# Moving eight gate columns of a decoder layer from the opening projection to the value projection of the forgetting heads

## The chip, the core and the metric

The kernel runs on one core of a Trainium2 chip. The metric is the device time of one execution in microseconds (us). A core has a matrix unit (TensorE, PE in the profile, with its weight loads as PEld), three engines for everything elementwise (VectorE or DVE, ScalarE or ACT, GpSimd or POOL) and SyncE (SP), which here issues the loads of weights and inputs. Matmul results land in PSUM, in banks of 2 KB per partition; there are eight of them. Everything else lies in SBUF, 128 partitions wide. Each engine works off its own instructions in order and waits on semaphores for the others.

## The reference

One decoder layer for 512 tokens, model width 1024: two attention branches on the same modulated input, a gated merge, an output projection, and a gated MLP with a depthwise convolution. The part that matters here:

```python
mod = c @ w_ada + b_ada                       # six vectors of 1024: shifts, scales, gates
u = x * (1.0 + sc1) + sh1
proj = u @ w_in
q_a, k_a, v_a, f_a, q_b, k_b, v_b, g_a, g_b = jnp.split(proj, ...)   # a: forgetting, b: stick-breaking

log_f = jax.nn.log_sigmoid(f_a + b_forget)    # 8 columns of proj, one for each forgetting head
cum = jnp.cumsum(log_f, axis=-1)              # along the tokens
logits = q_a k_a^T / 8 + cum[q] - cum[k]      # causal, then softmax and times v_a: forgetting attention
...                                           # b: stick-breaking attention, strictly causal
merged = sigmoid(g_a) * (y_fox @ w_fox_proj) + sigmoid(g_b) * (y_sb @ w_sb_proj)
x = layer_norm(ALPHA * x + (1.0 + gt1) * (merged @ w_o), ln1_g, ln1_b)
...                                           # gated MLP on x * (1 + sc2) + sh2, second layer norm
```

`f_a` is 8 columns wide. These are the "gate columns" below: the logits of the forget gate. The heads are 64 wide, eight of each kind.

## The kernel before

**Products.** All matrix products are float32 in accuracy: each operand is split into a high part (a rounded copy, on ScalarE: `hi_of`, L100) and a low part (the difference, on VectorE: `lo_of`, L103), and each product is three matmuls, high by high, high by low, low by high. Names end in h and l accordingly: `uh`/`ul` (the modulated input u, transposed, 8 tiles of 128 model rows by 512 tokens), `wh`/`wl` (weights). `mm3` (L140) issues the three.

**The opening.** Eight steps j, one for each 128 rows of the model width. SP loads for each step two tiles `wa` (128x1024 columns of w_ada), one `w1` tile `raw` (six bias columns, then 904 weight columns: q, k and q of the first stick-breaking heads, 3 x 128, the 512 value columns of the stick-breaking heads, 8 gate columns) and `xt` (128x512 of x). VectorE makes two sums over `wa` times c (`mod_col`, L216, with an addition of a bias column each, L211 and L212; POOL copies the bias columns to `bcols`, L285), ScalarE makes `uh` from `xt` (L302), and x itself turns into u in place (L304); VectorE subtracts for `wl` and `ul`. TensorE adds each step into eight groups `grp[0..7]`, one for each of the eight PSUM banks, which stay open over all eight steps: groups 0 to 2 are q, k, q (three matmuls each, weights standing still, 512 tokens moving), groups 3 to 6 the four token blocks by 512 value columns (three each), and group 7 the gate logits, two matmuls each: there the standing operand is `fpad[:, j, :]`, 128 columns, with the high parts of the gate columns in columns 0 to 7, the low parts in 64 to 71 and zeros elsewhere. So a step has 23 matmuls of 512 columns (L330). In the last step the groups that are wanted first are finished first, and groups 2 and 7 come between the first scores.

**Behind the opening.** Attention heads come in the order of `PAIRS`: four pairs of stick-breaking heads, then four of forgetting heads. TensorE's work between a head's steps is taken from one long list, `stream`: projections of q and k of later pairs (`proj`), the value projection of the forgetting heads (`vproj`, four token blocks of 24 matmuls of 512 columns, just ahead of pair 4, the first forgetting pair), the branch gates, the branch projections. `fill(n)` takes n matmuls or so from it, `fill_to(mark)` all up to a mark. The weights of these come as `items` of 128x1024 in four `raw` buffers, and are split to high and low when their turn nears; the value weights are four such items (`v_proc`), each of two 512-column tiles. A pool `z` of 60 buffers of 2 KB per partition serves most tiles.

**The gate.** `forget_evac`, right behind the opening, copies group 7 out of PSUM: rows 64 to 71 and rows 0 to 7 (with b_forget added) to two tiles `fq` of 8 rows by 512 tokens. While the seventh head runs (n == 6), `forget` adds the two, forms log sigmoid as min(x, 0) plus Ln(Sigmoid(Abs(x))) and the running sum with a scan, and splits it into the tile `chi`. From there POOL issues the transfers of `decay_rows`: for each forgetting head, its two rows of `chi` to rows 66 and 67 of `s2t[n]` and to rows 64 and 65 of `m2t[n]`. These two tiles are operands of the head's second score products: `scores` (L522 and L523) takes for each group of query blocks a first product of `s1` and `m1` (128 rows: high q twice against high and low k) and a second of `s2` and `m2` (64 rows and the four extra ones, whose products add cum[q] - cum[k] to the logits). The rows 0 to 63 of `s2t` come from `s1` by a transfer that POOL issues too.

**What sets the order.** SP's loads stand in the order written. For the other engines the order comes from the list scheduler, from estimated times; where `chain` is on (in the opening and up to the second head's scores), the instructions of an engine stay in the order of the program, through the wrapper `Pinned`, whose calls carry line L70. `tc.issue_after` puts an instruction behind another one.

## Time and profile before

| | |
|---|---|
| median of 3 runs | 754.06 us (753.83 to 754.61) |
| profiled execution, its own time | 753.64 us |
| its span in the trace | 751.5 us |
| mean granted TensorE clock | 0.997 |
| busy: PE, DVE, ACT, POOL | 99%, 73%, 47%, 17% of the span |
| moved by DMA | 100.46 MB, 134 GB/s on average |
| opening's matmuls | 179 at L330 and 5 at L70, of 3502 |

The span runs from the first to the last instruction that the profiler recorded; the execution's own time is 2.1 us more. Rows of a timeline give the start in the span, the length, the engine, the line, the operation, its result and operands (result<-operands), the tile of weights (partitions x columns) where there is one, shapes and the count; in square brackets stands the idle time ahead of the row and what ended it. Rows of groups give the line, engine, operation, tiles, count, the shortest, mean and longest in ns and the time of the first and last. L103 or L140 are lines of helpers, so that such rows are told apart by their tiles. A window's row gives for TensorE, its weight loads, VectorE, ScalarE, POOL and SP the busy time and the count, then TensorE's clock, the share of the DMA engines that was busy and GB/s.

### The profile page before, as it was taken

To read this page: it belongs to the slowest core of one execution; us is meant where nothing else is said; L and a number is where in the kernel's file an instruction comes from. 1 tells how busy PE (TensorE), PEld (TensorE's weight loads), DVE (VectorE), ACT (ScalarE), POOL (GpSimd) and SP (SyncE) were. 2 spreads that over 40 slices of the span, in tenths; PEclk is the share of its full clock that TensorE was granted. 3 is DMA by queue.
4 is the path that set the end of the run, shared out by engine and by line. 5 is a ranking of instruction groups with operands and counts; after the bars stand their busy time and mean duration, and the time that the engine had idled before them with its cause. 6 is when DMAs were issued, how large, how long until landed. Compare 5 with 4: busy or idle time off the path is not lost.

```text
span 751.5 us, 9515 instructions
## 1 busy us (share of the span) xinstructions
PE 741.8 (99%) x3502; PEld 621.0 (83%) x3502; DVE 545.4 (73%) x896; ACT 351.9 (47%) x587; POOL 126.6 (17%) x153
## 2 busy tenths in 40 slices
PE   9999999999999999999999999999999999999995
PEld 7888888888888888888898888888888888888885
DVE  7888989867688875596987787666755686334666
ACT  5578767468655754343246344444444442212300
POOL 2103000030110000000000690000000137454400
PEclk9999999999999999999999999999999999999998
DMA  9941332424333434565234524333333234224102
GB/s 352 405 142 70 99 139 87 157 84 168 106 114 120 154 113 168 169 232 165 86 113 140 168 94 131 139 114 133 120 117 107 85 110 149 104 86 140 56 33 79
DMA packets 31088, 100.46 MB, mean 134 GB/s; under 512 B 4113, under 2 KB 4641, under 8 KB 31042
## 3 DMA queue, kind: packets, MB, share of 16 engines
q1 hardware_dynamic: 29536, 97.69, 37.3%
q0 software_dynamic: 1504, 2.17, 1.2%
q8 instruction: 27, 0.44, 0.2%
q14 instruction: 19, 0.16, 0.1%
q10 hardware_dynamic: 2, 0.00, 0.0%
HBM read 96.63 MB, written 2.11 MB: 131 GB/s over the span
## 4 chain that ended last, share of the span: by engine, by line
PE 97%; DVE 2%; DMA 0%; ACT 0%; issue 0%; DVEq 0%
PE ps L140 56%; PE ps L330 5%; PE ps L1086 5%; PE ps L1084 5%; PE ps L1085 5%; PE ps L613 3%; PE ps L70 2%; PE ps L585 2%; PE ps L795 2%; PE ps L796 2%; PE ps L794 2%; PE ps L523 1%; PE ps L522 1%; PE ps L496 1%; PE ps L497 1%; PE ps L498 1%
## 5 line engine op out<-in xcount | busy, mean ns | idle before, releaser
L103 DVE TENSOR_TENSOR wl<-raw,wh 128x1024 fp32r<-128x1024 f32 (+1 forms) x99 | 133.2, 1346 | 55.4 <-ACT wh L100 55.2
L140 PE MATMUL ps<-u2h,wh 128*128 128x512 f32 (+1 forms) x376 | 141.2, 376 | 0.0
L140 PE MATMUL ps<-u2l,wh 128*128 128x512 f32 (+1 forms) x376 | 141.0, 376 | 0.0
L140 PE MATMUL ps<-u2h,wl 128*128 128x512 f32 (+1 forms) x376 | 133.6, 376 | 0.0
L100 ACT ACTIVATE wh<-raw 128x1024 fp32r<-128x1024 f32 (+1 forms) x99 | 103.5, 1048 | 62.7 <-PE ps L1086 46.1
L140 PE MATMUL ps<-uh,wh 128*128 128x512 f32 x213 | 84.1, 395 | 0.0
L140 PE MATMUL ps<-ul,wh 128*128 128x512 f32 x213 | 83.3, 391 | 0.0
L140 PEld LDWEIGHTS ps<-u2h,wh 128*128 128x128 f32 x376 | 70.8, 188 | 12.9
L140 PEld LDWEIGHTS ps<-u2l,wh 128*128 128x128 f32 x376 | 70.8, 188 | 12.6
L140 PEld LDWEIGHTS ps<-u2h,wl 128*128 128x128 f32 x376 | 70.4, 188 | 12.9
L140 PE MATMUL ps<-uh,wl 128*128 128x512 f32 x213 | 78.9, 390 | 0.0
L683 POOL TENSOR_TENSOR raw<-raw,gt 128x1024 f32<-128x1024 f32 x22 | 56.4, 2571 | 92.6 <-DMA raw<-in_wdn 85.0
L1057 DVE SCALAR_TENSOR_TENSOR cv<-ps,cw,cv 128x511 f32<-128x511 f32 x44 | 32.9, 748 | 53.4 <-ACT cv L1056 53.4
L1056 ACT ACTIVATE cv<-ps,cw 128x512 f32<-128x512 f32 x44 | 34.1, 776 | 45.7 <-PE ps L140 45.7
L1084 PE MATMUL ps<-wh,hh 128*128 128x512 f32 x128 | 49.8, 389 | 0.0
L1085 PE MATMUL ps<-wl,hh 128*128 128x512 f32 x128 | 49.8, 389 | 0.0
L1086 PE MATMUL ps<-wh,hl 128*128 128x512 f32 x128 | 49.8, 389 | 0.0
L140 PEld LDWEIGHTS ps<-uh,wl 128*128 128x128 f32 x213 | 40.0, 188 | 8.7
L140 PEld LDWEIGHTS ps<-uh,wh 128*128 128x128 f32 x213 | 40.0, 188 | 8.0
L140 PEld LDWEIGHTS ps<-ul,wh 128*128 128x128 f32 x213 | 40.1, 188 | 7.9
L100 ACT ACTIVATE hh<-cv 128x512 fp32r<-128x512 f32 x22 | 13.9, 633 | 57.5 <-DVE cv L1064 57.5
L216 DVE SCALAR_TENSOR_TENSOR ada<-ada,cbc 128x1024 f32<-128x1024 f32 x24 | 29.3, 1219 | 9.1 <-DMA ada<-in_wa 8.7
(245 smaller groups left out, 1428.7 us busy)
## 6 DMA issues: line engine op xcount, KB each, us to landing
raw<-in_wup SPq DMA_DIRECT2D x44, 512.0 KB, 3.4
raw<-in_wct SPq DMA_DIRECT2D x29, 512.0 KB, 3.8
ada<-in_wa SPq DMA_DIRECT2D x24, 512.0 KB, 4.3
raw<-in_wdn SPq DMA_DIRECT2D x22, 512.0 KB, 3.3
wa<-in_wa SPq DMA_DIRECT2D x16, 512.0 KB, 7.4
raw<-in_wp SPq DMA_DIRECT2D x8, 512.0 KB, 3.3
raw<-in_wo SPq DMA_DIRECT2D x8, 512.0 KB, 4.0
raw<-in_wa SPq DMA_DIRECT2D x8, 512.0 KB, 3.3
```

What stands on the lines that cost most here:

```text
L100: S.activation(o, i, AF.Copy, scale=scale)
L103: return V.tensor_tensor(o, i, fl(hi), ALU.subtract)
L140: PE.matmul(ps, w, u, start=first and n == 0, stop=last and n == 2)
L216: V.scalar_tensor_tensor(wt, wt, 1.0, cbc, ALU.mult, ALU.mult, accum_out=raw)
L330: PE.matmul(grp[g], w, u, start=j == 0 and n == 0, stop=j == KT - 1 and n == (1 if g == 7 else 2))
L613: PE.matmul(ps[:, to : to + w], v_part(br, h, j), src[e][:, so : so + w], start=a == 0 and j == 0, stop=a == 1 and j == 3)
L683: G.tensor_tensor(r, r, gt[1], ALU.mult)
L1056: S.activation(t, ps, AF.Identity, bias=cw[:, n, 3:4], scale=cw[:, n, 2:3])
L1057: V.scalar_tensor_tensor(t[:, 1:], ps[:, 0:511], cw[:, n, 1:2], t[:, 1:], ALU.mult, ALU.add)
L1084: PE.matmul(ps, hh[j][:, tb], w[0], start=first, stop=False)
L1085: PE.matmul(ps, hh[j][:, tb], w[1], start=False, stop=False)
L1086: PE.matmul(ps, hl[j][:, tb], w[0], start=False, stop=last)
```

## The change

The eight gate columns leave `w1` (`W1C` 904 to 896). They go into the value weights of the forgetting heads: each row of `wv` is now 256 value columns, 8 gate columns, 256 value columns (`VW` = 520), and the loads, the four `raw` buffers and the split tiles widen accordingly. Group 7 and `fpad` are gone, and with them the two gate matmuls of each step, the small copy on ScalarE and the small subtraction on VectorE; a tile of zeros `zpad` takes the place of `fpad` in the first two matmuls of the program. Of the two sums over `wa` for step j + 1, sum 0 moves ahead of `ul` of step j (`mod_sum` and `mod_add` are now apart). Among the scores of the first head stands group 6 instead of group 7.

`vproj` now takes each token block in two halves, of 264 and of 256 columns, each with 24 matmuls and a PSUM bank of its own; ScalarE copies the last 8 columns of the first half (tokens by heads, 128x8) to a tile `fgt`. `forget_evac` becomes an item of the stream, behind q of pair 4: four TensorE transposes turn `fgt` into heads by tokens in one PSUM bank, and ScalarE copies 8 rows of it with the bias to rows 96 to 103 of `chi`, which is now 104 rows by 512; the two `fq` are rows 64 and 96 of it, the high rows 0 to 7 and the low rows 32 to 39. The addition of the two parts is gone; the rest of `forget` is as it was. The memsets of the two `m2z` tiles are written ahead of the opening.

```diff
-W1C = 904
+W1C = 896
+VW = 512 + 8
-NZ = 60
+NZ = 59
-    fpad = early.tile([P, KT, P], F32R, name="fpad", tag="fpad")
+    zpad = early.tile([P, 512], F32R, name="zpad", tag="zpad")
...
-            it[3] = stg.tile([P, 1024], F32, name=nm("raw"), tag="raw", bufs=LOADS)
+            it[3] = stg.tile([P, 2 * VW], F32, name=nm("raw"), tag="raw", bufs=LOADS)
...
     def first_acc(j):
         wa = pend[j][0]
         G.tensor_copy(bcols[:, :, j], pend[j][2][:, 0:6])
-        mod_col(0, j, wa[0])
-        return mod_col(2, j, wa[1])
+        if j == 1:
+            mod_sum(0, j, wa[0])
+        mod_sum(2, j, wa[1])
+        mod_add(0, j)
+        return mod_add(2, j)
...
     def first_mod(j):
-        state["after"] = lo_of(b, xt, a)
-        with tc.issue_after(state["after"].ins):
-            hi_of(fpad[:, j, 0:NH], r[:, f])
-            state["pad"] = lo_of(fpad[:, j, 64 : 64 + NH], r[:, f], h[:, f])
+        if j + 1 < KT:
+            with tc.issue_after(state["split"].ins):
+                early_sum = mod_sum(0, j + 1, pend[j + 1][0][0])
+            with tc.issue_after(early_sum.ins):
+                state["after"] = lo_of(b, xt, a)
+        else:
+            state["after"] = lo_of(b, xt, a)
...
     def first_ops(j, g):
-        if g == 7:
-            return [(fpad[:, j, :], a), (fpad[:, j, :], b)]
...
+    m2z = [z(F32R, "m2z", (68, 512)) for _ in range(2)]
+    for t in m2z:
+        G.memset(fl(t[64:68, :]), 0.0)
+
     for j in range(2):
         first_load(j)
...
-            first_mm(j, range(5, 8))
+            first_mm(j, range(5, 7))
         else:
-            first_mm(j, (0, 1, 3, 4, 5, 6))
+            first_mm(j, (0, 1, 3, 4, 5))
...
-        chi.append(att.tile([NH, 2, 512], F32R, name="chi", tag="chi"))
+        chi.append(att.tile([96 + NH, 512], F32R, name="chi", tag="chi"))
...
+    def forget_open():
+        fgt.append(atp[0].tile([P, NB * NH + P], F32, name="fgt", tag="fgt"))
+        G.memset(fgt[0][:, NB * NH :], 0.0)

     def forget_evac():
-        S.activation(fq[0], grp[7][64 : 64 + NH, :], AF.Copy)
-        S.activation(fq[1], grp[7][0:NH, :], AF.Identity, bias=bfs)
+        fq.extend(fl(chi[0][r : r + NH, :]) for r in (64, 96))
+        ps = bank()
+        for j in range(NB):
+            PE.transpose(ps[:, j * P : (j + 1) * P], fgt[0][:, j * NH : j * NH + P], ident)
+        S.activation(fq[1], ps[0:NH, :], AF.Identity, bias=bfs)
+        return
+        yield

     def forget(after):
         with tc.issue_after(after.ins):
-            V.tensor_tensor(fq[1], fq[1], fq[0], ALU.add)
             S.activation(fq[0], fq[1], AF.Abs)
...
-        G.dma_start(s2t[n][66:68, :], chi[0][h : h + 1, :, :])
-        G.dma_start(m2t[n][64:66, :], chi[0][h : h + 1, :, :])
+        G.dma_start(s2t[n][66:68, :], chi[0][h : h + 33 : 32, :])
+        G.dma_start(m2t[n][64:66, :], chi[0][h : h + 33 : 32, :])
...
-    def vproj(j, last):
-        ps = bank()
+    def vproj(j, half, last):
+        c = slice(0, 264) if half == 0 else slice(264, VW)
+        bk = bank()
+        ps = bk[:, 0 : c.stop - c.start]
...
         for k in range(KT):
-            h, l = wvs[k]
+            h, l = [w[:, c] for w in wvs[k]]
             PE.matmul(ps, uh[k][:, tb], h, start=k == 0, stop=False)
             PE.matmul(ps, uh[k][:, tb], l, start=False, stop=False)
             PE.matmul(ps, ul[k][:, tb], h, start=False, stop=k == KT - 1)
-            yield 3
-        for half in range(2):
-            v_evac(0, j, half, ps)
+            yield 1.5
+        v_evac(0, j, half, bk[:, 0:256])
+        if half == 0:
+            S.activation(fgt[0][:, j * NH : (j + 1) * NH], bk[:, 256:264], AF.Copy)
...
                 if c == "q":
                     add_wv(p)
+                    if p == 4:
+                        stream.append((forget_evac, ()))
...
             for j in range(NB):
-                stream.append((vproj, (j, wvi[-1])))
+                for half in range(2):
+                    stream.append((vproj, (j, half, wvi[-1])))
...
-    first_mm(KT - 1, (7,))
+    first_mm(KT - 1, (6,))
...
-    forget_evac()
     q_evac(1, 1, grp[2])
```

VectorE's order in the opening, one step, before: the wide subtraction, `ul`, the small gate subtraction, then the two sums over `wa` of the next step with their additions.

```order
L103 TENSOR_TENSOR wl_193<-raw_137,wh_192 128x904
L103 TENSOR_TENSOR ul_212<-xt_138,uh_211 128x512
L103 TENSOR_TENSOR fpad<-raw_137,wh_192 128x8
L216 SCALAR_TENSOR_TENSOR wa_179,modr<-wa_179,cbc 128x1024
L216 SCALAR_TENSOR_TENSOR wa_180,modr<-wa_180,cbc 128x1024
L211 TENSOR_TENSOR modc<-modr,bcols 128x1
L212 SCALAR_TENSOR_TENSOR modc<-modr,bcols 128x1
```

The same step on VectorE now (the lines have moved by one or two):

```order
L104 TENSOR_TENSOR wl_194<-raw_140,wh_193 128x896
L214 SCALAR_TENSOR_TENSOR wa_180,modr<-wa_180,cbc 128x1024
L104 TENSOR_TENSOR ul_213<-xt_141,uh_212 128x512
L214 SCALAR_TENSOR_TENSOR wa_181,modr<-wa_181,cbc 128x1024
L210 TENSOR_TENSOR modc<-modr,bcols 128x1
L211 SCALAR_TENSOR_TENSOR modc<-modr,bcols 128x1
```

The first of the two sums now stands between the wide subtraction and `ul`, and the small subtraction is gone.

VectorE's order around the gate's rows, before: the minimum (L396), the scan (L397) and the subtraction for `chi`, with other heads' and sums' rows between them (`fq_522` and `fq_523` are the two `fq`, `yf` and `yl` belong to an earlier head's output).

```order
L396 SCALAR_TENSOR_TENSOR fq_523<-fq_523,fq_522 8x512
L620 TENSOR_TENSOR yf_1507<-ps_1623,ytmp_1632 64x512
L397 SCALAR_TENSOR_TENSOR fq_522<-ones,fq_523 8x512
L212 SCALAR_TENSOR_TENSOR modc<-modr,bcols 128x1
L103 TENSOR_TENSOR yl_1636<-yf_1507,yh_1635 128x512
L103 TENSOR_TENSOR chi<-fq_522,chi 8x512
```

Now, with the subtractions of the first two forgetting heads' `m` rows (`m_0`, `m_1`: `m2t`) and a weight subtraction `wl` between:

```order
L104 TENSOR_TENSOR wl_1812<-raw_1322,wh_1811 128x1024
L409 SCALAR_TENSOR_TENSOR chi<-chi 8x512
L410 SCALAR_TENSOR_TENSOR chi<-ones,chi 8x512
L104 TENSOR_TENSOR m_0_541<-ps_1810,m_356_1841 64x512
L104 TENSOR_TENSOR wl_1851<-raw_1726,wh_1850 128x1024
L104 TENSOR_TENSOR m_1_542<-ps_1810,m_357_1845 64x512
L104 TENSOR_TENSOR chi<-chi 8x512
```

The subtraction for `chi` came before the first forgetting heads' k was projected; now it comes behind both subtractions of that projection's result.

TensorE's order at the scores of the first forgetting head, before (`s_347` and `m_353` are `s1` and `m1`, `s_0` and `m_0` are `s2t[0]` and `m2t[0]`): the first products (L522) and the second ones (L523) alternate.

```order
L140 MATMUL ps_1774<-uh_258,wl_1698 128x512
L522 MATMUL ps_1810<-m_353_1766,s_347_1727 128x256
L523 MATMUL ps_1810<-m_0_576,s_0_572 128x256
L522 MATMUL ps_1810<-m_353_1766,s_347_1727 128x256
L523 MATMUL ps_1810<-m_0_576,s_0_572 128x256
L522 MATMUL ps_1815<-m_353_1766,s_347_1727 128x384
L523 MATMUL ps_1815<-m_0_576,s_0_572 128x384
L522 MATMUL ps_1818<-m_353_1766,s_347_1727 128x512
L523 MATMUL ps_1818<-m_0_576,s_0_572 128x512
```

Now three first products (L539) stand ahead:

```order
L539 MATMUL ps_1884<-m_356_1841,s_349_1796 128x256
L539 MATMUL ps_1889<-m_356_1841,s_349_1796 128x384
L539 MATMUL ps_1892<-m_356_1841,s_349_1796 128x512
```

and 29 rows later on TensorE the second ones (L540) with the first product that was left:

```order
L141 MATMUL ps_1958<-ul_213,wh_1811 128x512
L540 MATMUL ps_1884<-m_0_541,s_0_537 128x256
L539 MATMUL ps_1884<-m_356_1841,s_349_1796 128x256
L540 MATMUL ps_1884<-m_0_541,s_0_537 128x256
L540 MATMUL ps_1889<-m_0_541,s_0_537 128x384
L540 MATMUL ps_1892<-m_0_541,s_0_537 128x512
L141 MATMUL ps_1958<-uh_212,wl_1812 128x512
```

The two products no longer follow each other: 20 matmuls of projections and 9 transposes of earlier heads' weights stand between.

More of the change, by code (lines that the diff above doesn't have):

```diff
@@ L106, in layer_kernel @@
     cbr = early.tile([97, D], F32, name="cbr", tag="cbr")
-    fpad = early.tile([P, KT, P], F32R, name="fpad", tag="fpad")
+    zpad = early.tile([P, 512], F32R, name="zpad", tag="zpad")
     bcols = const([P, 6, KT], F32, "bcols")
     nc.scalar.dma_start(cbr[96:97, :], crow)
-    V.memset(fl(fpad[:, KT - 4 : KT, :]), 0.0)
+    V.memset(fl(zpad), 0.0)
     for c in (slice(0, 256), slice(256, D)):
@@ L193, in layer_kernel @@
     pend = {}
-    G.memset(fl(fpad[:, 0 : KT - 4, :]), 0.0)
     def zeros(n):
         for _ in range(n):
-            PE.matmul(grp[3], fpad[:, KT - 1, :], fpad[:, KT - 4 : KT, :], start=True, stop=True)
+            PE.matmul(grp[3], zpad[:, 0:P], zpad, start=True, stop=True)
     chain["on"] = True
@@ L212, in mod_end, with mod_sum, mod_add @@
         return V.scalar_tensor_tensor(o, raw, 1.0, b, ALU.add, ALU.add)
+    def mod_sum(w, col, wt):
+        return V.scalar_tensor_tensor(wt, wt, 1.0, cbc, ALU.mult, ALU.mult, accum_out=modr[:, w, col, 0:1])
+    def mod_add(w, col):
+        return mod_end(w, col, modr[:, w, col, 0:1], bcols[:, w, col : col + 1])
     def mod_col(w, col, wt):
-        raw = modr[:, w, col, 0:1]
-        V.scalar_tensor_tensor(wt, wt, 1.0, cbc, ALU.mult, ALU.mult, accum_out=raw)
-        return mod_end(w, col, raw, bcols[:, w, col : col + 1])
+        mod_sum(w, col, wt)
+        return mod_add(w, col)
     def first_load(j):
         wa = [early.tile([P, D], F32, name=nm("wa"), tag="wa", bufs=5) for _ in range(2)]
-        r = stg.tile([P, 1024], F32, name=nm("raw"), tag="raw", bufs=LOADS)
+        r = stg.tile([P, 2 * VW], F32, name=nm("raw"), tag="raw", bufs=LOADS)
         xt = z(F32, "xt")
@@ L265, in first_zero @@
         sh, sc = modc[:, 0, 0:1], modc[:, 2, 0:1]
-        lo, hi, f = slice(0, 384), slice(384, W1C), slice(W1C - NH, W1C)
+        lo, hi = slice(0, 384), slice(384, W1C)
         G.tensor_copy(bcols[:, :, 0], r[:, 0:6])
@@ L273, in first_zero @@
         S.activation(cbc[:, c], cq, AF.Copy)
-        hi_of(fpad[:, 0, 0:NH], r[:, f])
         lo_of(l[:, lo], r[:, lo], h[:, lo])
         lo_of(l[:, hi], r[:, hi], h[:, hi])
-        lo_of(b, xt, a)
-        state["after"] = lo_of(fpad[:, 0, 64 : 64 + NH], r[:, f], h[:, f])
+        state["after"] = lo_of(b, xt, a)
         pend[0][2:] = [h, l]
@@ L292, in first_split @@
         hi_of(h[:, 0:W1C], r)
-        lo_of(l[:, 0:W1C], r, h[:, 0:W1C])
+        state["split"] = lo_of(l[:, 0:W1C], r, h[:, 0:W1C])
         pend[j][2:] = [h, l, r]
@@ L297, in first_mod @@
         xt = pend[j][1]
-        h, l, r = pend[j][2:]
         sh, sc = modc[:, 0, j : j + 1], modc[:, 2, j : j + 1]
-        f = slice(W1C - NH, W1C)
         a, b = z(F32R, "uh"), z(F32R, "ul")
@@ L327, in first_mm @@
         if j < KT - 1:
-            ops.sort(key=lambda o: o[1] + 3 * (o[0] == 7))
+            ops.sort(key=lambda o: o[1])
         for g, n, (w, u) in ops:
-            PE.matmul(grp[g], w, u, start=j == 0 and n == 0, stop=j == KT - 1 and n == (1 if g == 7 else 2))
+            PE.matmul(grp[g], w, u, start=j == 0 and n == 0, stop=j == KT - 1 and n == 2)
+    m2z = [z(F32R, "m2z", (68, 512)) for _ in range(2)]
+    for t in m2z:
+        G.memset(fl(t[64:68, :]), 0.0)
     for j in range(2):
@@ L359, in layer_kernel @@
     ORD = (1, 0, 2, 3)
-    m2z = [z(F32R, "m2z", (68, 512)) for _ in range(2)]
-    for t in m2z:
-        G.memset(fl(t[64:68, :]), 0.0)
     ptc, s2t, m2t, chi, atp = [], [], [], [], []
@@ L397, in forget @@
         V.tensor_tensor_scan(fq[0], ones[0:NH, 0:1].broadcast_to([NH, 512]), fq[1], 0.0, ALU.mult, ALU.add)
-        hi_of(chi[0][:, 0, :], fq[0])
-        lo_of(chi[0][:, 1, :], fq[0], chi[0][:, 0, :])
+        hi_of(chi[0][0:NH, :], fq[0])
+        lo_of(chi[0][32 : 32 + NH, :], fq[0], chi[0][0:NH, :])
         gated.append(True)
@@ L471, in v_evac @@
         v3 = vv.rearrange("s (p q d) -> s p q d", q=4, d=64)
-        p3 = ps[:, half * 256 : (half + 1) * 256].rearrange("s (p q d) -> s p q d", q=2, d=64)
+        p3 = ps.rearrange("s (p q d) -> s p q d", q=2, d=64)
         hi_of(v3[:, :, 0::3, :], p3)
@@ L482, in v_proc @@
         for e in range(2):
-            h, l = z(F32R, "wvh"), z(F32R, "wvl")
-            hi_of(h, r[:, e * 512 : (e + 1) * 512])
-            lo_of(l, r[:, e * 512 : (e + 1) * 512], h)
+            h, l = z(F32R, "wvh", (P, VW)), z(F32R, "wvl", (P, VW))
+            c = slice(e * VW, (e + 1) * VW)
+            hi_of(h, r[:, c])
+            lo_of(l, r[:, c], h)
             wvs.append((h, l))
     wvs = []
-    def vproj(j, last):
-        ps = bank()
-        weights(last, AHEAD if j == NB - 1 else 0)
+    def vproj(j, half, last):
+        c = slice(0, 264) if half == 0 else slice(264, VW)
+        bk = bank()
+        ps = bk[:, 0 : c.stop - c.start]
+        weights(last, AHEAD if (half, j) == (1, NB - 1) else 0)
         tb = slice(j * P, (j + 1) * P)
         for k in range(KT):
-            h, l = wvs[k]
+            h, l = [w[:, c] for w in wvs[k]]
             PE.matmul(ps, uh[k][:, tb], h, start=k == 0, stop=False)
@@ L845, in layer_kernel @@
     lim[0] = marks["y1"]
-    chain.update({"on": True, S: state["u"], V: state["pad"]})
+    chain.update({"on": True, S: state["u"], V: state["after"]})
     weights(0, 0)
@@ L1150, in _pack @@
     first = [w_in[:, s : s + P] for s in (col("q", 0), col("k", 0), col("q", 1))]
-    cols = np.concatenate([bcol] + first + [w_in[:, 2568:3080], w_in[:, 1536:1544]], axis=1)
+    cols = np.concatenate([bcol] + first + [w_in[:, 2568:3080]], axis=1)
     w1 = c(cols.reshape(KT, P, W1B))
```

16 lines of the change are left out of this document (9 added, 7 removed).

## The prediction

> **What bounds the kernel now.** I read the page first (busy shares, granted clock, chain), then TensorE's timeline by place, then the engines that feed it.
>
> ```profile
> span 751.5 us, 9515 instructions
> PE 741.8 (99%) x3502; PEld 621.0 (83%) x3502; DVE 545.4 (73%) x896; ACT 351.9 (47%) x587; POOL 126.6 (17%) x153
> PEclk9999999999999999999999999999999999999998
> PE 97%; DVE 2%; DMA 0%; ACT 0%; issue 0%; DVEq 0%
> ```
>
> TensorE is busy for 99% of the span, at full clock in every slice but the last, and is 97% of the chain that ended last. So the time is a sum over matmuls, plus a few waits; work on other engines counts only where TensorE waits for it. A busy row's length is no price (they overlap): I take spacings from start to start. TensorE's timeline, at both ends of the opening and at the program's end:
>
> ```profile
> 13.35 0.39 PE L330 MATMUL ps<-ul,fpad 128*128 128x512 f32 x1
> 13.68 0.96 PE L330 MATMUL ps<-uh,wh 128*128 128x512 f32 x3
> ...
> 39.89 0.84 PE L330 MATMUL ps<-uh,wh 128*128 128x512 f32 x3
> ...
> 45.11 0.39 PE L330 MATMUL ps<-uh,wh 128*128 128x512 f32 x1
> ...
> 742.05 0.28 PE L1086 MATMUL ps<-wdh,hl 128*128 128x256 f32 x1
> ...
> 743.49 0.28 PE L1086 MATMUL ps<-wdh,hl 128*128 128x256 f32 x1
> ```
>
> One opening step (39.89 to 45.11) is 23 matmuls: 0.227 us for 512 columns. The twelve of 256 columns from 742.05 to 743.49, each with weights of its own, stand 0.120 apart.
>
> **Opening, what goes away.** Two gate matmuls in each of eight steps: 16 x 0.227 = **-3.63 us**, all on the chain, if TensorE is still fed. First VectorE's rows of one step, then what gates the second step (rows of VectorE, POOL and ScalarE, the same POOL copy for the eighth step, and a row of the window table, which ends in the share and GB/s of the transfers):
>
> ```profile
> 35.14 1.22 DVE L216 SCALAR_TENSOR_TENSOR wa<-wa,cbc 128x1024 f32<-128x1024 f32 x1
> 36.28 1.22 DVE L216 SCALAR_TENSOR_TENSOR wa<-wa,cbc 128x1024 f32<-128x1024 f32 x1
> 37.62 1.10 DVE L103 TENSOR_TENSOR wl<-raw,wh 128x904 fp32r<-128x904 f32 x1
> 39.44 0.69 DVE L103 TENSOR_TENSOR ul<-xt,uh 128x512 fp32r<-128x512 f32 x1 [0.71 <-ACT xt L304]
> 40.13 1.22 DVE L216 SCALAR_TENSOR_TENSOR wa<-wa,cbc 128x1024 f32<-128x1024 f32 x1
> ```
> ```profile
> 11.23 1.22 DVE L216 SCALAR_TENSOR_TENSOR wa<-wa,cbc 128x1024 f32<-128x1024 f32 x1
> 11.60 0.90 POOL L285 COPY bcols<-raw 128x6 f32<-128x6 f32 x1 [4.51 <-DMA raw<-in_w]
> 12.54 0.16 DVE L211 TENSOR_TENSOR modc<-modr,bcols 128x1 f32<-128x1 f32 x1
> 12.81 0.82 ACT L302 ACTIVATE uh<-xt,modc 128x512 fp32r<-128x512 f32 x1 [0.18 <-DVE modc L212]
> 38.84 0.19 POOL L285 COPY bcols<-raw 128x6 f32<-128x6 f32 x1 [3.65 <-DMA raw<-in_w]
> 20.00:25.00 5.00, 5.00 (x24) 4.14 (x23) 4.29 (x10) 2.94 (x5) 1.39 (x2) 1.00 1.03 404
> ```
>
> VectorE's step is 40.13 - 35.14 = 4.99 us, 0.71 of it a wait for ScalarE's xt. TensorE's new step is 21 x 0.227 = 4.77, so the old VectorE step would be too slow. The moved sum fills that wait, and the gate's small subtraction goes: two sums 2.3 (1.14 from start to start), two adds 0.2 (36.28 + 1.14 to 37.62), the wide subtraction 1.1, ul 0.7, in all 4.3. The loads of a step (3462 columns of 128 rows, 1.77 MB; each w1 tile is only 4 KB smaller) need 4.39 us at the 404 GB/s of the window row. Both are under 4.77, and the last weight tile, there at 38.84, is wanted by the eighth step, six steps of 4.77 behind 13.6, at about 42.2. Eight tiny ScalarE copies go with the step and cost nothing either way. The POOL memsets of m2z move ahead of the opening, where POOL has nothing that TensorE waits for; SP's loads keep their order.
>
> The second step is the exception: it starts when its uh is there (12.81 + 0.82 = 13.63; TensorE was free at 13.58 and waited 0.10). Now TensorE is free 0.45 earlier, but uh hangs on the sum at 11.23 and on the POOL copy at 11.60, which waits for a load and ended (12.50) just after that sum. One VectorE operation less ahead of it brings uh some 0.09 forward: the wait becomes 0.46, **+0.36 us** (bounds 0 and +0.45).
>
> **Behind the opening, a bank.** The eighth group no longer holds a PSUM bank, so the first stick-breaking scores get one more to rotate over.
>
> ```profile
> 51.00 0.33 PE L70 MATMUL ps<-m2z,s 68*128 68x384 f32 x1
> 51.47 0.50 PE L70 MATMUL ps<-m,s 128*128 128x512 f32 x1
> 52.43 0.28 PE L70 MATMUL ps<-m2z,s 68*128 68x256 f32 x1
> 52.73 0.50 PE L70 MATMUL ps<-uh,wh 128*128 128x512 f32 x1
> 53.07 0.40 PE L70 MATMUL ps<-ul,wh 128*128 128x512 f32 x1
> 51.04 0.39 ACT pt L70
> ```
>
> On the line between 0.120 and 0.227 a 384-column matmul takes 0.174. So 51.00 to 51.47 holds a wait of 0.30, 52.43 to 52.73 one of 0.18, and the matmul behind such a wait is slow by 0.11 (52.73 to 53.07), twice: 0.70. The chain goes through ScalarE's pt at 51.04, which empties the bank. With a further bank I take **-0.60 us** (bounds 0 and -0.70).
>
> **The value projection** goes from 96 matmuls of 512 columns to 96 of 264 and 96 of 256. On that line (0.107 us for 256 columns more) 264 columns cost 0.1233. 96 x (0.1233 + 0.120 - 0.227) = **+1.57 us**, all TensorE. Bounds: 264 priced as 256 gives +1.25; as 384 gives +6.4. I stay on the line since 256 is next to it. Twice the weight loads are in the 0.120 already. The halves take eight banks instead of four, emptied by the same copy and subtraction as before plus a 128x8 copy; counted in the order with these spacings, TensorE comes back to such a bank 5.7 us or more after it left it, and that other matmul work hides the emptying. If it didn't, TensorE would wait at those transposes.
>
> The fixed part of a matmul is by these rows 2 x 0.120 - 0.227 = 0.013 us. The Trainium skill (TensorE: Matmul & The Clock Gate, "Wait — 56ns, not 53.3ns?") gives N / 2.4 GHz + 2.5 ns from start to start, 0.1092 us for 256 columns, 0.1125 for 264, 0.2157 for 512. By that the split would cost 96 x 0.0060 = +0.58 us by estimate, and the whole sum would be -2.6. The trace's 0.120 and 0.227 say otherwise.
>
> **Four transposes** more, in the stream between q and k of the first forgetting pair.
>
> ```profile
> 59.13 1.25 PE L70 MATMUL ps<-idz,pt 128*128 128x128 f32 x10
> 60.14 0.48 PE L70 MATMUL ps<-uh,wh 128*128 128x512 f32 x1
> ```
>
> Ten take 1.01 us (59.13 to 60.14): 4 x 0.101, and 0.05 for a slow start of the next matmul, half of the 0.11 above: **+0.45 us** (bounds 0.40 and 0.51).
>
> **A wait that comes in.** The gate's rows used to be copied out right behind the opening and were worked off beside the seventh head. Now that work starts behind the transposes, and the first forgetting head's second score products need its result, through a POOL transfer. What it takes (groups of the tiles fq and chi, then timeline rows, then the landing of chi's transfers):
>
> ```profile
> L393 ACT ACTIVATE fq<-fq x1: 615/615/615, 146.8 to 146.8; 8x512 f32<-8x512 f32 x1
> L396 DVE SCALAR_TENSOR_TENSOR fq<-fq,fq x1: 670/670/670, 155.1 to 155.1; 8x512 f32<-8x512 f32 x1
> L397 DVE TENSOR_TENSOR_SCAN fq<-ones,fq x1: 1214/1214/1214, 156.5 to 156.5; 8x512 f32<-8x512 f32 x1
> L103 DVE TENSOR_TENSOR chi<-fq,chi x1: 681/681/681, 158.5 to 158.5; 8x512 fp32r<-8x512 f32 x1
> 150.72 1.28 ACT L395 ACT_TABLE_LOAD   x1
> 161.18 1.20 ACT L100 ACTIVATE s<-ps 64x512 fp32r<-64x512 f32 x2
> 162.28 1.05 ACT L100 ACTIVATE wh<-raw 128x1024 fp32r<-128x1024 f32 x1
> 159.45 0.77 POOL L411 DMA_DIRECT2D s<-chi  x1 [13.01 <-DVE chi L103]
> 163.79 1.07 POOL L434 DMA_DIRECT2D s<-s  x2
> 163.85 1.23 DVE L103 TENSOR_TENSOR wl<-raw,wh 128x1024 fp32r<-128x1024 f32 x1
> DMA to landing us min/median/max: 1.6/2.3/4.8
> ```
>
> From the end of q's projection: ScalarE does q's two halves (1.2), the gate's copy (0.6), a weight copy (1.0), three functions (3 x 0.62) and the table load (1.28), to 6.0 us; VectorE the minimum and the scan (1.95), to 8.0; then its queue holds m's subtraction, a weight subtraction, m's second one and chi's (0.7 + 1.2 + 0.7 + 0.7), to 11.2; POOL's first issue (0.77), to about 11.9, where the m rows' transfer is issued; landed 1.6 to 4.8 later, at 13.5 to 16.7, 14.2 by the median. TensorE, by the order (53 matmuls of 512 columns, three score products, 14 transposes), is there at 14.1. So the wait is 0 to 2.6 us, **+0.20** taken: nearest the median. Behind it TensorE's whole queue stands. In POOL's queue the two transfers of q's halves go ahead of chi's now; they are free to go at 1.2, so they cost nothing. The softmax of that head comes some 4 us later, but TensorE wants it only some 10 us behind its scores.
>
> **Sum.** -3.63 + 0.36 - 0.60 + 1.57 + 0.45 + 0.20 = -1.65. The profiled execution took 753.64 us (span 751.5 and 2.1 around it), so 752.0; the median of the runs is 0.42 above it: **752.4 us**, 0.22% less. About 0.2% (1.5 us) is what timing can tell from no change, and the forecast lies on that edge.
>
> **Rivals.**
> - *The decay rows land late.* At the largest landing the wait is 2.6: 752.4 + 2.4 = 754.8. For it: by the median there is no slack, and the weight subtraction ahead of chi's frees a buffer, so that a 512 KB load is under way at the same time. Against: half of the landings take 2.3 or less.
> - *The opening is fed too slowly.* If VectorE stays at 4.99 a step (a sum that waits for its load ahead of ul), seven steps gain 0.23 each, not 0.45: 1.5 us lost, 753.9. For it: the moved sum needs a later load. Against: 4.3 and 4.39 stand under 4.77.
> - *Slower: POOL's issues are blocked.* The bcols copy took 0.90 instead of 0.19 beside a VectorE sum. If an issue also had to wait until VectorE's instruction ends, the two issues for this head would come behind the ptc split and the 1.22 us sum that follow chi: some 2.2 us later, and with a landing of 4.8 the wait is 4.8: 757.0. It decides from a wait of 3.4 us, that is from m rows landed 17.5 us after q's projection. Against: the two issues at 163.79 took 1.07 beside VectorE's subtraction of two SBUF tiles at 163.85. This is the rule of the Trainium skill (SBUF — State Buffer, "SBUF: two separate sides"): while VectorE holds the shared port pair, GpSimd can't write its transfers' descriptors; the trace doesn't bear it out at that place.
> - *The split is cheaper*: if the fixed 0.013 us hides behind the pair that shares its weights, only 8 columns more are paid, 96 x 8 x 0.00042 = 0.32 us: 751.1. Against it stand the rows of 0.120, where every second and third matmul shares an operand too.
>
> **Chances.** Forecast 0.55 (751.7 to 753.1), late rows 0.18, slow opening 0.12, cheaper split 0.09, slower 0.06. Faster by over 0.2%: the cheaper split and nearly four fifths of the forecast, 0.52; slower 0.06; same 0.42. Range 751.2 to 754.2, which leaves out the worst landings and the slower case.
>
> **What would show it.** The opening's steps at 4.77 from the second on, with a wait near 0.46 ahead of 13.6; no gap like 51.00 to 51.47; 264- and 256-column rows at 0.123 and 0.120; TensorE's first second-product of the forgetting scores starting without idle time. Wrong if a VectorE or DMA releaser appears ahead of L334 rows, or a POOL transfer ahead of the scores.

## The result, and the profile after

The changed kernel takes **766.39 us** (median of 4 runs, 765.87 to 767.44) against 754.34 (753.83 to 754.64) for the kernel before: a ratio of 1.0163, 95% interval 1.0151 to 1.0175. It is 12 us slower; 752.4 was forecast. The profiled execution took 766.23 us with a span of 764.5, 13.0 more than before, at a mean granted TensorE clock of 0.998.

The head of the page after:

```profile
span 764.5 us, 9664 instructions
...
PE 753.3 (99%) x3586; PEld 623.5 (82%) x3586; DVE 546.6 (71%) x887; ACT 351.7 (46%) x582; POOL 128.1 (17%) x153
...
PEclk9999999999999999999999999999999999999999
...
PE 94%; DVE 2%; DMA 1%; ACT 1%; SPq 0%; issue 0%; POOL 0%; DVEq 0%; ACTq 0%
```

TensorE is as busy as before, at the same granted clock, and still carries the chain; behind the start of the program its longest wait is 1.3 us. The time is in the spacing of the matmuls, in stages that the change doesn't touch. TensorE's timeline in the up-projection of the MLP, before and then after (start, length):

```profile
450.16 0.39 PE L140 MATMUL ps<-u2h,wh 128*128 128x512 f32 x1
450.39 0.39 PE L140 MATMUL ps<-u2l,wh 128*128 128x512 f32 x1
450.61 0.39 PE L140 MATMUL ps<-u2h,wl 128*128 128x512 f32 x1
450.84 0.39 PE L140 MATMUL ps<-u2h,wh 128*128 128x512 f32 x1
```
```profile
449.90 0.40 PE L141 MATMUL ps<-u2h,wh 128*128 128x512 f32 x1
450.14 0.39 PE L141 MATMUL ps<-u2l,wh 128*128 128x512 f32 x1
450.37 0.39 PE L141 MATMUL ps<-u2h,wl 128*128 128x512 f32 x1
450.60 0.40 PE L141 MATMUL ps<-u2h,wh 128*128 128x512 f32 x1
```

Three matmuls took 0.68 us before and take 0.70 now. In nanoseconds the three steps are 227, 226, 227 before and 238, 230, 232 after, the same triple again and again. Over the whole program the mean spacing of matmuls of 512 columns is 227.41 ns before and 232.51 after (steps under 260 ns between two such matmuls): 2704 of them times 5.1 are 13.8 us, which is more than the whole loss.

The decay rows, which the prediction priced at 0.20, cost more as well. TensorE at the first forgetting head's second score products:

```profile
172.24 0.40 PE L141 MATMUL ps<-ul,wh 128*128 128x512 f32 x1
173.95 0.36 PE L540 MATMUL ps<-m,s 68*128 68x256 f32 x1 [1.32 <-DMA m<-chi]
```

From start to start this is 1.71 us where 0.23 is usual: a wait of 1.48.

### The profile page after: what moved, and what is told of

Read it like the earlier page. It is cut to its first block, busy times and chain, and to the rows that moved or that the text cites. A ratio compares the mean times of both kernels' runs of the same rounds, so it can differ in the third digit from the quotient of the medians.

```text
span 764.5 us, 9664 instructions
## 1 busy us (share of the span) xinstructions
PE 753.3 (99%) x3586; PEld 623.5 (82%) x3586; DVE 546.6 (71%) x887; ACT 351.7 (46%) x582; POOL 128.1 (17%) x153
## 4 chain that ended last, share of the span: by engine, by line
PE 94%; DVE 2%; DMA 1%; ACT 1%; SPq 0%; issue 0%; POOL 0%; DVEq 0%; ACTq 0%
PE ps L141 55%; PE ps L1105 5%; PE ps L1103 5%; PE ps L1104 5%; PE ps L334 4%; PE ps L630 3%; PE ps L71 3%; PE ps L814 2%; PE ps L813 2%; PE ps L815 2%; PE ps L602 2%; PE ps L540 1%; PE ps L539 1%; DMA raw<-in_w 1%; PE ps L514 1%; PE ps L512 1%
## 5 line engine op out<-in xcount | busy, mean ns | idle before, releaser
L141 PE MATMUL ps<-u2h,wh 128*128 128x512 f32 (+1 forms) x376 | 143.5, 382 | 0.0
L141 PE MATMUL ps<-u2h,wl 128*128 128x512 f32 (+1 forms) x376 | 135.7, 381 | 0.0
```

The source lines that it names most:

```text
L141: PE.matmul(ps, w, u, start=first and n == 0, stop=last and n == 2)
```

## The experiments

**What makes the spacing.** In the program as built, every operand tile of these matmuls starts, in the kernel before, 32 bytes behind a multiple of 512 bytes of its partition (all pools before it add up that way, and the slices that TensorE takes are 512 bytes apart). In the changed kernel the tiles of `z` are 2080 bytes apart instead of 2048, so that no two neighbours lie at the same place modulo 512, and u2h and u2l (128 behind such a multiple) no longer lie like the split weights (288). Theory A: that placement makes the spacing. Theory B: the order or number of TensorE's instructions does. Theory C: power or the clock.

First the pitch alone, in the kernel before:

```diff
-NZ = 60
+NZ = 59
-            h, l = z(F32R, "wvh"), z(F32R, "wvl")
+            h, l = [z(F32R, t, (P, 520))[:, 0:512] for t in ("wvh", "wvl")]
```

> The kernel before with one thing of the change alone: the tiles of the pool z take 2080 bytes per partition instead of 2048 (59 of them), as the wider value weights made them; no instruction is added, removed or widened. Theory A, placement: TensorE's matmuls of 512 columns start 227 ns apart where all their operands lie at the same place within 512 bytes (in the kernel before every one starts 32 bytes behind a multiple of 512), and 231 to 234 ns apart where they don't; then this kernel has the spacing of the changed one, and 2900 x 4 to 6 ns are 12 to 17 us: 766 to 771 us. Theory B, the order or the number of TensorE's instructions makes the spacing: 754 us and 227 ns, since they are the same here. Theory C, power or the clock: 754 us too, the work being the same.

Measured: 768.08 us (767.19 to 768.1), ratio 1.0183, interval 1.0168 to 1.0198. Its timeline at the same place:

```profile
450.05 0.39 PE L140 MATMUL ps<-u2h,wh 128*128 128x512 f32 x1
450.28 0.40 PE L140 MATMUL ps<-u2l,wh 128*128 128x512 f32 x1
450.52 0.39 PE L140 MATMUL ps<-u2h,wl 128*128 128x512 f32 x1
450.75 0.39 PE L140 MATMUL ps<-u2h,wh 128*128 128x512 f32 x1
```

0.70 us for three again, and a mean of 232.45 ns over the program. No instruction of the change is in this kernel; TensorE's instructions are those of the kernel before, in the same order, and its waits are the same two (1.4 us at the start, 0.2 at the layer norm), at a granted clock of 0.997. It has the whole loss. Theories B and C are out.

Then the other way round, the change with its tiles at one place:

```diff
-VW = 512 + 8
+VW = 512
...
-        c = slice(0, 264) if half == 0 else slice(264, VW)
+        c = slice(0, 256) if half == 0 else slice(256, VW)
...
-            S.activation(fgt[0][:, j * NH : (j + 1) * NH], bk[:, 256:264], AF.Copy)
+            S.activation(fgt[0][:, j * NH : (j + 1) * NH], bk[:, 248:256], AF.Copy)
...
-    wvg = np.concatenate([w_in[:, 1024:1280], w_in[:, 1536:1544], w_in[:, 1280:1536]], axis=1)
+    wvg = w_in[:, 1024:1536]
```

> The changed kernel with value-weight tiles of 512 columns: the gate's eight columns are left out of the product and the gate is made from eight value columns instead (the values of the gate are not the reference's; every instruction stays, only 264 columns become 256). All operand tiles then lie at 32 bytes behind a multiple of 512, as in the kernel before. Theory A, placement: spacing 227 ns again, and the time that the prediction's sum gives without the eight columns, 752.4 - 0.3 = 752.1 us, give or take 1.5. Theory B, the order or number of TensorE's instructions: spacing stays at 231 to 234 ns, about 766 us.

Measured: 753.28 us (752.47 to 754.22, 10 runs), ratio 0.9991, interval 0.9982 to 1.0001. The spacing is back to 227.37 ns:

```profile
450.16 0.39 PE L141 MATMUL ps<-u2h,wh 128*128 128x512 f32 x1
450.39 0.39 PE L141 MATMUL ps<-u2l,wh 128*128 128x512 f32 x1
450.62 0.39 PE L141 MATMUL ps<-u2h,wl 128*128 128x512 f32 x1
450.84 0.39 PE L141 MATMUL ps<-u2h,wh 128*128 128x512 f32 x1
```

The time is 1.2 us above the 752.1 expected. The wait for the decay rows, 1.49 in this trace where the sum had 0.20, accounts for that; it comes further down.

**Which places must agree.** Three buffers for the split weights take turns, one product (24 matmuls) each. Padding between them gives each its own place, with everything else left at 32:

```diff
-NZ = 60
+NZ = 59
...
+    OFFS = (0, 32, 160)
...
+            shape = [P, 1024 + (PADS[i] // 4 if t == "wl" else 0)]
+            out.append(stg.tile(shape, F32R, name=nm(t), tag=f"{t}{i}")[:, 0:1024])
...
+    PADS = [(OFFS[(i + 1) % 3] - OFFS[i]) % 512 for i in range(3)]
```

> The kernel before with padding between the three buffers of the split weights, so that wh and wl of a product start 32, 64 or 192 bytes behind a multiple of 512, in turn, while the other operands stay at 32 (the pool z has 59 tiles of 2048 bytes). Theory A: products of the first buffer keep 227 ns (those that follow another buffer's may take some to come back), those of the other two go to 230 to 234; two thirds of about 2000 matmuls x 5 ns are 7 us: 760 to 762 us. If only the place within 64 bytes counts, the second buffer (64) is slow and the third (192) too; if a shift of 160 is what the changed kernel suffers from, the third has a repeating 238, 230, 232 ns. Theories B and C: 754 us, 227 ns in all three.

Measured: 765.75 us in one run, 4 to 6 above what was expected. First matmuls of four products in a row, from the timeline:

```profile
450.73 0.40 PE L140 MATMUL ps<-u2h,wh 128*128 128x512 f32 x1
...
456.23 0.39 PE L140 MATMUL ps<-u2h,wh 128*128 128x512 f32 x1
...
461.82 0.40 PE L140 MATMUL ps<-u2h,wh 128*128 128x512 f32 x1
...
467.42 0.40 PE L140 MATMUL ps<-u2h,wh 128*128 128x512 f32 x1
```

The first product (buffer at 0) takes 5.50 us, the second (32 further on) 5.59, the third (160) 5.60; 24 steps of 226.67 ns would be 5.44. Within the first, the first nine steps behind the change of buffer are slow, the others are at 227. So a mismatch is paid at once, and here the agreement takes effect some matmuls later. That is the smaller part of the miss: the 1234 steps with operands alike are 0.94 ns slower than before on average, 1.2 us in all, while 1575 steps that are not alike cost 5.85 each, 9.2 us, where some 1330 times 5 were expected.

The next run put the buffers at 64, 128 and 256:

```diff
-    OFFS = (0, 32, 160)
+    OFFS = (64, 128, 256)
...
+        if not turn_of[0]:
+            stg.tile([P, 16], F32, name="lead", tag="lead")
...
-    PADS = [(OFFS[(i + 1) % 3] - OFFS[i]) % 512 for i in range(3)]
+    PADS = [64, 128, 256]
```

> As the run with three offsets, but wh and wl of a product lie 64, 128 or 256 bytes further on than the other operands (modulo 512). That run had 233.1 ns between matmuls for 32 bytes, 233.4 for 160, 226.7 for none. If every difference costs the same, all three buffers show 233 here and the time is about 754.1 + 2000 x 6.5 ns = 767 us. If only differences that are no multiple of 64 (or 128, or 256) bytes cost, the second and third buffer, or the third alone, stay at 226.7, and the time is 763 or 759 us, or 754 if all three stay.

Measured: 763.54 us in one run.

```profile
444.32 0.39 PE L140 MATMUL ps<-u2h,wh 128*128 128x512 f32 x1
...
449.76 0.40 PE L140 MATMUL ps<-u2h,wh 128*128 128x512 f32 x1
...
455.36 0.39 PE L140 MATMUL ps<-u2h,wh 128*128 128x512 f32 x1
...
460.94 0.39 PE L140 MATMUL ps<-u2h,wh 128*128 128x512 f32 x1
```

The product at 256 (444.32 to 449.76) takes 5.44 us, the one at 64 takes 5.60, the one at 128 takes 5.58. So the operands must agree modulo 256 bytes. The product at 256 has no slow start, though it follows the buffer at 128: its steps are 227, 227, 226 ns from the first on. The recovery of the run before doesn't come behind every mismatch. The mean spacings within products of the up-projection, both runs together: 228.8 ns at 0 (with the recovery), 233.1 at 32, 233.4 at 64, 232.3 at 128, 233.4 at 160, 226.8 at 256. In the down-projection, where the split weights are the moving operand and the others stand still, the same buffers give 229.6 (64), 232.8 (128) and 227.7 (256), so that 64 costs less there than in the up-projection. It isn't the one or the other operand that has to lie right; the two have to lie alike.

Last, all tiles moved together:

```diff
+    stg.tile([P, 8], F32, name="lead", tag="lead")
```

> The kernel before with 32 bytes of padding ahead of all buffers, so that all operand tiles lie 64 bytes behind a multiple of 512 instead of 32, still alike. If only the places relative to each other count: 754 us and 227 ns. If the place within 64 bytes itself counts (a tile of 2048 bytes now touches 32 blocks of 64 instead of 33): another spacing throughout, faster or slower, by 2 ns or more, 6 us.

Measured: 755.06 us in one run, a spacing of 227.35 ns. The timeline:

```profile
450.45 0.39 PE L140 MATMUL ps<-u2h,wh 128*128 128x512 f32 x1
450.68 0.39 PE L140 MATMUL ps<-u2l,wh 128*128 128x512 f32 x1
```

The place itself doesn't matter, at 32 or at 64. (The 0.9 us above the median of before: the first matmul of the opening starts 1.9 us later in this trace, at 10.07 instead of 8.19; SP's issue of the first `raw` tile takes 1.20 us there instead of 0.42, and TensorE waits 0.55 for a memset on POOL; what delays the issue is open.)

| kernel | mean step, operands alike modulo 256 | not alike | us |
|---|---|---|---|
| before | 227.41 ns x2813 | none | 754.1 |
| changed | 230.43 x37 | 232.54 x2667 | 766.4 |
| pitch alone | 229.51 x59 | 232.52 x2753 | 768.1 |
| change, aligned | 227.37 x2702 | none | 753.3 |
| offsets 0, 32, 160 | 228.35 x1234 | 233.26 x1575 | 765.8 |
| offsets 64, 128, 256 | 227.81 x1220 | 232.32 x1590 | 763.5 |
| all shifted by 32 | 227.35 x2810 | none | 755.1 |

These are steps under 260 ns between two matmuls of 512 columns, with the start addresses of the program as built; a step is alike if the operands of both its matmuls are. Matmuls of 256 columns don't show the loss: 209 steps between two of them average 121.1 ns in the kernel before, where all operands are alike, and 119.9 with the pitch alone, where none are.

**The change with its gate, aligned.** The 264-column halves must stay in one piece, and 16 of them (1056 bytes) don't fit beside 59 tiles of 2048. The first try gave them 15 tiles of their own and `z` 52 tiles:

```diff
-NZ = 59
+NZ = 52
...
+        return zp.tile([P, 264], F32R, name=nm(t), tag="w0", bufs=15)
...
+            own = [first_half(t) for t in ("wgh", "wgl")]
+            for (h, l), c in ((own, slice(0, 264)), ([w[:, e * 256 : (e + 1) * 256] for w in pair], slice(264, VW))):
```

> The changed kernel, gate and all, with every tile but the first halves of the value weights at one place modulo 512 bytes: the 264-column halves lie in 15 tiles of their own (1056 bytes) and one of z, the 256-column halves two to a tile of z, which has 52 tiles of 2048 bytes. Placement theory: spacing 227 ns outside the 96 matmuls of 264 columns, and the time of the aligned run without the gate's columns (753.28 us) plus 96 x 8 columns (0.3) plus up to 0.6 for the 192 matmuls beside the misplaced halves: 753.3 to 754.2. If 59 tiles were needed to keep the engines ahead, TensorE waits somewhere and the time is above 755.

> As the kernel beside it, but the four transposes and the copy of the gate stand right behind the value projection, ahead of q of the first forgetting pair, 24 matmuls earlier. In the changed kernel TensorE stood 1.49 us at the second score products of the first forgetting head, waiting for the transfer of the decay rows. If that chain alone makes the wait, moving it 24 x 0.227 = 5.4 us ahead ends it: 1.4 us less than the kernel beside it, 751.9 to 752.8. If something else is as late there (the transfer of q's rows, k's subtraction), or the copies now hold up TensorE at the transposes, less than half of it comes back.

Measured: 762.85 us (761.16 to 764.25) and 765.58 (764.29 to 766.42). The matmuls of 512 columns are at 227 ns in both (227.4 and 227.3 on average), and now waits carry most of the loss. TensorE's waits in the first of the two (what waited, for what, us in total, times, longest):

```profile
PE ps L1026 <- DVE xn L1016: 5.7, 1, 5.7
...
PE ps L551 <- DMA m<-chi: 1.2, 1, 1.2
PE ps L550 <- DVE pl L104: 1.1, 1, 1.1
```

In the second the wait for m<-chi is gone, and TensorE waits for the gate's copy at the transposes (2.9 us). So what the alignment brings is mostly lost again: the first kernel is 3.5 us faster than the changed one and 9 slower than before. Two things are new beside the alignment, fewer tiles in `z` and twice as many instructions for the split; these runs don't separate them. The early transposes trade one wait for another here, where ScalarE's copy stands behind VectorE's subtraction of the same half.

The wait was then tried by itself, in the aligned kernel without the gate's columns, with that copy moved ahead of the value columns and the transposes put behind the value projection instead of behind q of pair 4:

```diff
+        if half == 0:
+            S.activation(fgt[0][:, j * NH : (j + 1) * NH], bk[:, 248:256], AF.Copy)
         v_evac(0, j, half, bk[:, 0:256])
...
-                    if p == 4:
-                        stream.append((forget_evac, ()))
...
+            stream.append((forget_evac, ()))
```

> The aligned run without the gate's eight columns (753.28 us) with two moves: ScalarE copies the 8 gate columns ahead of the value halves instead of behind them, and the four transposes stand right behind the value projection, ahead of q of the first forgetting pair. In the aligned run TensorE waited 1.49 us for the decay rows at 172.26 us; in the kernel of the last batch with the early transposes that wait was gone, but TensorE waited 3.06 us at the transposes, for a copy that ScalarE made behind VectorE's subtraction. If the prediction's term for the decay rows is all that was wrong with its sum beside the placement: no wait at either place, 753.28 - 1.4 = 751.9 us. If the copy is still late, a wait of up to 3 us at the transposes and 753.5 to 755.

Measured: **751.67 us** (750.89 to 752.25), ratio 0.9965, interval 0.9953 to 0.9978. All that TensorE waits for in it:

```profile
PE ps L68 <- DVE zpad L111: 1.4, 1, 1.4
PE ps L71 <- POOL m2z L338: 0.6, 1, 0.6
PE ps L1014 <- DVE xn L1004: 0.2, 1, 0.2
```

The first two lie in the program's first four microseconds. There is no wait for decay rows and none at the transposes: 753.28 - 1.61. That is the sum of the prediction without its 0.20 for the rows and 0.3 for the gate's columns, 751.9, within 0.25 us.

For the whole computation the halves got a pool of 8 tiles of 2112 bytes, two halves in each, opened with the attention pools; its place is used again for the layer norm's xn:

```diff
-NZ = 59
+NZ = 52
...
+            (slice(0, 528), [atp[1].tile([P, 528], F32R, name=nm(t), tag="w0", bufs=8) for t in ("wgh", "wgl")]),
+            (slice(528, 1040), [z(F32R, t) for t in ("wvh", "wvl")]),
...
+        xn = [xnp.tile([P, 512], F32, name=nm("xn"), tag="xn", bufs=8) for _ in range(2)]
```

> The changed kernel, gate and all, with 264-column halves of the value weights in a pool of their own, two side by side in a tile (2112 bytes, eight tiles), so that the split takes as many instructions as in the changed kernel; 52 tiles of 2048 bytes in z, and the place of that pool is used again for the eight xn tiles of the first layer norm. In the run with 52 tiles and no such place TensorE waited 5.86 us at the layer norm's transposes and about 2.8 us between 125 and 146 us. If these waits were for want of tiles, and for the doubled split instructions: 753.28 + 0.3 for the eight columns, up to 0.6 for misplaced halves, 753.5 to 754.2 us, with 1.5 us of waiting for the decay rows still there. If 52 tiles are too few for the attention stage itself: waits remain between 125 and 146 us and the time is 755 to 757.

> The kernel beside it with the two moves of the early run (gate copy ahead of the value copies, transposes right behind the value projection). If both cures hold: the time of the kernel beside it less 1.4 us, 752.0 to 752.8, which is the prediction's 752.4 with its placement right, and faster than the kernel before by 0.2%. Otherwise as the kernel beside it, or slower by what TensorE waits at the transposes.

Measured: 754.23 us (753.54 to 755.62, 11 runs), ratio 1.0003, interval 0.9994 to 1.0012; and 756.02 (754.58 to 757.27), 1.0024, interval 1.0015 to 1.0033. The first is at the upper end of what was expected, the wait for the decay rows included; the wait of 5.7 at the layer norm is gone with the same 52 tiles in `z`, so that no larger `z` is needed for it. The second missed: two waits came up that the narrow kernel hadn't had, one of them again for ScalarE's copy at the transposes (L400); their cause was not followed further:

```profile
PE ps L607 <- DVE modc L211: 1.7, 1, 1.7
...
PE ps L400 <- ACT fgt L522: 1.4, 1, 1.4
```

So the transposes went back, and the rows behind them were hastened instead: `forget` called right behind the transposes, chi's high part on VectorE, k's subtractions behind chi's, and 34 (or 38) matmuls of the stream ahead of the first forgetting head's scores:

```diff
+        forget(hd[(1, 7)]["last"])
...
-        hi_of(chi[0][0:NH, :], fq[0])
-        lo_of(chi[0][32 : 32 + NH, :], fq[0], chi[0][0:NH, :])
+        V.tensor_copy(chi[0][0:NH, :], fq[0])
+        state["chi"] = lo_of(chi[0][32 : 32 + NH, :], fq[0], chi[0][0:NH, :])
...
-        lo_of(m2[0:64, :], ps[r, :], m1[0:64, :])
+        with tc.issue_after(state["chi"].ins) if (br, p) == (0, 0) else nullcontext():
+            lo_of(m2[0:64, :], ps[r, :], m1[0:64, :])
...
-                fill(LEAD)
-                f1 -= LEAD
-            if n == 6:
-                forget(hd[heads[n + 1]]["last"])
+                lead = LEAD if n != 6 else 34
+                fill(lead)
+                f1 -= lead
```

> The aligned kernel with the gate (754.23 us, 1.41 of it TensorE's wait for the decay rows, which were issued by POOL at 170.08 us and landed some 4.2 later) with the rows made earlier and wanted later: the high part of chi is copied on VectorE instead of ScalarE, the low part follows at once, k's subtractions for the first forgetting pair come behind it, and 34 instead of 6 projection matmuls stand ahead of the first forgetting head's scores. By the rows of that run chi is ready 2.1 us earlier (the scan ends at 165.8, two short instructions on VectorE 1.3), so the m rows land at about 172.2, and TensorE comes to them at about 173.4: no wait. If the wait is all that is left of the difference to the prediction's sum: 754.23 - 1.4 = 752.8 us, 0.998 to 0.999 of before. If the softmax of that head, now later, is waited for instead: no gain.

> As the kernel beside it with 38 matmuls ahead of these scores instead of 34: the same time if neither the rows nor the softmax are late; slower by up to 0.9 us if the softmax is.

Measured: **752.61 us** (751.62 to 754.09, 9 runs), ratio 0.9977, interval 0.9967 to 0.9987; with 38, 752.93 (751.06 to 754.71, 11 runs), 0.9982, interval 0.9974 to 0.9991. Both are faster than the kernel before (by 0.2%, the interval clear of 1) and than the changed one. VectorE, POOL and TensorE in the first:

```profile
166.43 0.42 DVE L413 CAST chi<-chi 8x512 fp32r<-8x512 f32 x1
166.88 0.68 DVE L104 TENSOR_TENSOR chi<-chi 8x512 fp32r<-8x512 f32 x1
...
168.43 0.55 POOL L427 DMA_DIRECT2D m<-chi  x1
...
172.72 0.28 PE L546 MATMUL ps<-m,s 128*128 128x256 f32 x1
172.83 0.29 PE L547 MATMUL ps<-m,s 68*128 68x256 f32 x1
```

The m rows land at 170.06 here, 1.63 us behind their issue, and TensorE takes its second product at 172.83 without idling. (The expectation had put the landing in the kernel of 754.23 us 4.2 us behind the issue; by its trace it was 2.75, 170.08 to 172.83. The rows here came earlier than forecast, and the margin is larger.)

## Why the prediction was wrong

The step that failed is the first one: "so the time is a sum over matmuls", priced by the spacings of before, 0.227 for 512 columns. That the tiles of `z` grow by 32 bytes was taken as a matter of space and got no term. It changed the price of nearly every matmul of 512 columns (2667 of the 2704 steps) by 5 ns, 13 to 14 us, more than all terms of the sum together. None of the four rivals has it; the case "slower" got 0.06 for another reason. The prediction had the spacing in its own list of what would show it right or wrong only for the opening's steps (4.77 forecast, 4.84 to 4.89 in the changed kernel from the third on).

The terms, measured in the aligned kernels, where that price is as before:

- *Gate matmuls, -3.63, the second step, +0.36, the bank, -0.60.* TensorE reaches the first ten transposes at 55.31 instead of 59.13, -3.82 against -3.87 forecast. The steps of the opening are 4.76 us long (37.62 to 42.38 below, in the aligned run without the gate's columns; 4.77 forecast), so VectorE and the loads keep up, and the slow opening didn't come. The second step starts at 13.68 in both, so uh came no earlier at all (+0.45, the bound; VectorE's chain to it began 0.09 later in this trace), and the bank waits vanish altogether: what is left of the 3.82 for them is 0.64.

```profile
37.62 0.84 PE L334 MATMUL ps<-uh,wh 128*128 128x512 f32 x3
...
42.38 0.39 PE L334 MATMUL ps<-uh,wh 128*128 128x512 f32 x1
...
55.31 1.25 PE L71 MATMUL ps<-idz,pt 128*128 128x128 f32 x10
```

- *Value projection, +1.57.* In the aligned kernel with the gate (754.23 us; there 80 of the 96 matmuls of 264 columns still have operands that aren't alike), matmuls of 264 columns stand 0.1238 apart, of 256 columns 0.1194 (forecast 0.1233 and 0.120). But those of 512 columns in the value projection before stood 0.2311 apart on average, not 0.227, so the split cost 23.35 - 22.19 = 1.16 us. The cheaper split (264 columns near the price of 256 and a hidden fixed part) didn't come: 0.0044 us lie between them. The rule of the Trainium skill that the prediction weighed (TensorE: Matmul & The Clock Gate, "Wait — 56ns, not 53.3ns?") gives 0.1125 and 0.1092, by estimate; the trace has 0.1238 and 0.1194 and doesn't agree.
- *Transposes, +0.45.* In the changed kernel four of them take 158.14 to 158.49, 0.35, and the next matmul is 0.09 slow: 0.44.
- *Decay rows, +0.20.* Right in kind, mis-sized: 1.48 in the changed kernel. The chain there, on ScalarE, VectorE and POOL:

```profile
158.14 0.60 PE L399 MATMUL ps<-idz,fgt 128*128 128x128 f32 x4
...
165.40 1.22 DVE L410 TENSOR_TENSOR_SCAN chi<-ones,chi 8x512 f32<-8x512 f32 x1
...
167.37 1.20 ACT L101 ACTIVATE m<-ps 64x512 fp32r<-64x512 f32 x2 [0.42 <-DVE m L104]
168.59 0.63 ACT L101 ACTIVATE chi<-chi 8x512 fp32r<-8x512 f32 x1
169.33 0.68 DVE L104 TENSOR_TENSOR chi<-chi 8x512 fp32r<-8x512 f32 x1
...
170.88 0.55 POOL L425 DMA_DIRECT2D m<-chi  x1
```

The m rows are issued 12.74 us behind q's projection (11.9 forecast: ScalarE's copy of chi stands behind its two copies of m, which the sum left out; its 1.95 for the minimum and the scan is 1.88 by the rows that it shows) and land 2.93 later, at 173.81 (2.3 taken, 1.6 to 4.8 given). That is 15.67 behind q's projection instead of 14.2: 0.84 and 0.63 make the 1.47 between. TensorE was there at 14.33 (14.1 forecast). The rival of late rows was thus the nearer one there. That POOL's issues would be blocked by VectorE's instructions is not borne out: its two issues for this head start 0.3 us and 0.9 us behind the end of chi's subtraction, each 0.55 to 0.58 long, the second beside VectorE's subtraction for ptc; and two later ones, at 173.56 and 174.09, take 0.54 each beside VectorE's 1.23 us sum that starts at 173.59.

All terms together, without the gate's columns and the wait, come within 0.25 us of the run of 751.67 us, which doesn't separate them. The whole change with its operands aligned (but for the 264-column halves) and its order kept (754.23) lies 1.8 us above the forecast 752.4, and the wait for the decay rows is 1.3 of that: even without the placement, the gain that was forecast would not have come.

## What to carry to other kernels

A change of a tile's width moves every tile allocated behind it: before pricing a kernel that is bound by TensorE with matmuls of 512 columns, list the start addresses of its operands modulo 256 bytes, before and after. Keep pool pitches at multiples of 256 bytes (or pad, or give the odd tiles a pool of their own whose size is such a multiple), and when every matmul of a program is slower by the same few ns at the same granted clock, look at placement ahead of waits. The whole change, rightly placed and with its rows in time, was worth 1.7 us here (754.27 to 752.61); the 32 bytes cost 13.

## What the runs showed of the hardware

Matmuls of 512 float32 columns with weights of their own run 226.67 ns apart where the moving operand and the weights start at the same place modulo 256 bytes of the partition, and in the up-projection 232 to 234 ns apart on average where they differ by 32, 64, 128 or 160 bytes (in the down-projection 232.8 at 128 and 229.6 at 64). Matmuls of 256 columns show no such loss (121.1 ns alike, 119.9 not). The price comes at once; the cure came nine steps later behind a buffer at 160 and at once behind one at 128. In the kernel before, 2415 of the 2813 steps are 226 or 227 ns; an eighth of all are slower although all operands agree, most of them between 50 and 300 us, where scores and other work stand between, for instance behind products of 68 rows; what sets that off, and why 256 bytes are the period, no run here shows. The Trainium skill (SBUF — State Buffer, "Operand start alignment") asks of an operand only that it start at a multiple of its element size, and says that its runs timed nothing; the kernels here keep to that, and the pitch alone costs 1.8%.
